# The up-projection of a feed-forward block as seven half-size products (Strassen's scheme), in three token blocks instead of two

## The chip, the cores and the metric

The kernel runs on one core of one Trainium2 chip. The metric is the device time in microseconds (us) of one execution; lower is better. The chip's engines run beside each other, each with its own queue in program order: TensorE (PE in the profile) multiplies matrices into PSUM, VectorE (DVE), ScalarE (ACT) and GpSimd (POOL) work elementwise, and transfers are queued by SyncE (SP) or POOL.

## What is computed

One layer of a hybrid decoder over 2048 prompt tokens and 8 x 8 sample tokens. Three mixers read one combined projection, their outputs are projected, added and layer-normed to x1; then comes a gated feed-forward block. The change is in that last block alone (and in how x1 is laid out for it):

```python
def conv_ffn(x, buf, w_up, conv_w, conv_b, w_down):
    up = x @ w_up                                   # 1024 -> 2 * 2816
    gate, val = jnp.split(up, [D_FF], axis=-1)
    gate, buf_new = causal_dwconv(gate, buf, conv_w)    # width 3, along the tokens
    h = jax.nn.gelu(gate + conv_b) * val
    return h @ w_down, buf_new                      # 2816 -> 1024
...
    f, fconv_new = conv_ffn(x, st_fconv, ffn_w_up, ffn_conv_w, ffn_conv_b, ffn_w_down)
    x = layer_norm(ALPHA * x + f, ln2_g, ln2_b)
```

All of it is float32. Every float32 product is made of three single passes (`mm3`): both operands are split into a rounded part (h, type fp32r) and the rest (l), and h\*h, l\*h and h\*l are added up in PSUM. To split is one ACT cast (h) and one subtraction on DVE or POOL (l = source - h).

## The kernel before

`program` (L1946) runs four stages: `phase1` (the combined projection), `window_a` (mixer A), `window_c` (mixer C beside the output projection, `Project`) and `phase3` (the feed-forward block). In `phase3` the program order is the order of the code (`manual_schedule`); each engine takes its instructions in that order.

**Tiles and loops.** The 2112 tokens are two blocks (`FB`): 1024 tokens, and 1024 + 64. The 2816 hidden columns are 22 tiles of 128 (`NH`). For each block and each hidden tile, `hidden` makes the gate rows and the value rows of the tile: a gate and a value product for each chunk of the block's tokens (512, 512 in the first block, 384, 384, 320 in the second), each product 8 steps of 128 in K by 3 passes, so 24 matmuls (`up`, PSUM tiles pug and puv, six banks in all). ACT copies the gate from PSUM to G (L1695), `conv` applies the three taps (one ACT activation L1713 and two DVE scalar_tensor_tensor L1715 to act) and the gelu (L1717), DVE multiplies with the value out of PSUM (L1748), ACT rounds to hh (L1749), DVE makes hl (L1757).

**Down-projection.** Hidden tiles are taken in pairs (`GRP` = 2). The products of a pair with `w_down` (`down`, PSUM tile pd, two banks) are queued behind the up-products of the tile that follows the pair: for each 128 tokens and each half of the 1024 columns, 2 x 3 matmuls, and one DVE add of the bank to Y (L1866 the first time, L1868 after). So the order on PE is: products of an even tile, down-products of the pair before it, products of the odd tile, products of the next even tile, and so on. I call the products of one tile P and one such run of down-products D. The tail of the even tile (the multiplication, hh, hl) is queued amid D's adds. A pair waits in hh and hl.

**Weights.** Weights are streamed for each block: `more` splits the next weight tile of 1024 columns (ACT cast L1605, POOL subtraction L1606 to wl_g, wl_v, wl_d) and queues the load of a later one on SP. The order `keys` is made ahead.

**Block change.** `load_x` (L1657 to L1659) loads and splits the tokens of a block in eight steps amid the down-products of the last pair of the block before. The second layer norm of a finished block (`stats`, `ln_scale`, `apply` L1779, `store`) is a list `todo`, from which `side` takes two or three entries at places in the next block's first tiles. `load_y` loads the x1 tile to which the down-products are added.

## Time and profile before

| | before |
|---|---|
| median of 3 runs | 3038.6 us (3037.53 to 3039.21) |
| profiled execution, its span | 3039.2 us |
| PE busy | 2895.7 us (95%), 17755 matmuls |
| DVE busy | 1597.9 us (53%) |
| ACT busy | 1231.6 us (41%) |
| POOL busy | 843.4 us (28%) |
| moved to and from memory | 80 GB/s over the span |

The profiled execution took as long as the runs (0.6 us over the median). PE, DVE and so on are engines, L1606 is a line of the kernel; a row names the line, the engine, the operation and the tiles as output<-inputs. In a timeline each row begins with the start and the duration in us, "x8" means eight instructions in a row merged, and a bracket holds the idle time before and what ended it. In the chain of waits, each row has the start, the time spent and the line. In a table of stages (windows) each engine has its busy time and, after x, its instructions; PEclk is the granted clock of TensorE, 1.00 at full speed. Matmuls are pipelined: their pace is read from the distance of two starts, not from one duration.

### The profile page before, as it was taken

What the parts mean: (1) busy time and instruction counts of PE and PEld (TensorE: products, weight loads), DVE (VectorE), ACT (ScalarE), POOL (GpSimd) and SP (SyncE); (2) the same over time, 40 slices, a digit from 0 to 9 for tenths busy, and PEclk for the clock granted to TensorE, in tenths of its full rate; (3) what the DMA queues carried; (4) which work ended last, traced back from release to release, by engine and by line L of the source; (5) the groups of instructions that cost most, each with busy time, mean ns of one, the idle gap of its engine ahead of it and who ended that gap; (6) DMA issues with size and microseconds to landing.
All of it is one profiled execution on the core that took longest, in us unless ns stands there. A gap on an engine that the chain in (4) does not pass through costs nothing.

```text
span 3039.2 us, 44833 instructions
## 1 busy us (share of the span) xinstructions
PE 2895.7 (95%) x17755; PEld 2496.9 (82%) x17755; DVE 1597.9 (53%) x2654; ACT 1231.6 (41%) x2591; POOL 843.4 (28%) x892
## 2 busy tenths in 40 slices
PE   8999999789889899998899999999999999999998
PEld 7888789678778677776678888888889999999997
DVE  4564442587665688978533333333366444334446
ACT  4474443446665567756332222222232222222223
POOL 0000001734523545434322222222232222222224
PEclk9999999689898679999999999999999999999999
DMA  6221112433433333322431111111124111111111
GB/s 197 83 74 70 56 61 100 137 106 107 123 99 91 81 120 109 111 82 87 160 123 50 49 42 63 42 56 42 49 104 152 42 47 51 49 42 42 48 43 62
DMA packets 182106, 247.20 MB, mean 81 GB/s; under 512 B 37986, under 2 KB 147640, under 8 KB 181832
## 3 DMA queue, kind: packets, MB, share of 16 engines
q1 hardware_dynamic: 179768, 237.02, 24.2%
q0 software_dynamic: 1984, 7.12, 0.6%
q8 instruction: 140, 2.29, 0.3%
q14 instruction: 70, 0.57, 0.1%
q10 hardware_dynamic: 144, 0.20, 0.0%
HBM read 183.94 MB, written 60.08 MB: 80 GB/s over the span
## 4 chain that ended last, share of the span: by engine, by line
PE 79%; DVE 10%; ACT 4%; issue 3%; DMA 2%; POOL 2%; SPq 0%; POOLq 0%; ACTq 0%; DVEq 0%
PE pm L320 20%; PE pd L320 15%; PE pug L320 15%; PE puv L320 15%; PE s L1364 2%; PE zp L1121 1%; DVE Tm L897 1%; DVE y L1779 1%; DVE tmp L895 1%; DVE K L1337 1%; PE zp L1122 1%; ACT WU L920 1%; PE zp L1123 1%; PE pd L1861 1%; DMA fxl<-s_x1T 1%
## 5 line engine op out<-in xcount | busy, mean ns | idle before, releaser
L1715 DVE SCALAR_TENSOR_TENSOR act<-G,cols,act 128x1024 f32<-128x1024 f32 (+1 forms) x132 | 123.6, 950 | 493.5 <-ACT act L1713 491.1
L1868 DVE TENSOR_TENSOR y<-y,pd 128x512 f32<-128x512 f32 x322 | 220.9, 687 | 203.3 <-PE pd L320 196.8
L1606 POOL TENSOR_TENSOR wl_d<-ws_d,wh_d 128x1024 fp32r<-128x1024 f32 x44 | 106.2, 2415 | 571.3 <-ACT wh_d L1605 547.3
L320 PE MATMUL pd<-wh_d,hh 128*128 128x512 f32 x704 | 215.8, 391 | 4.4 <-DVE y L1868 2.6
L320 PE MATMUL pd<-wh_d,hl 128*128 128x512 f32 x704 | 215.4, 391 | 0.0
L320 PE MATMUL pd<-wl_d,hh 128*128 128x512 f32 x704 | 214.9, 390 | 0.0
L1695 ACT COPY G<-pug 128x512 f32<-128x512 f32 (+2 forms) x110 | 55.2, 503 | 386.3 <-PE pug L320 386.3
L320 PE MATMUL pug<-fxh,wh_g 128*128 128x512 f32 (+2 forms) x880 | 197.0, 352 | 5.3 <-ACT fxh L1658 2.7
L320 PE MATMUL pug<-fxl,wh_g 128*128 128x512 f32 (+2 forms) x880 | 196.6, 352 | 2.5 <-POOL fxl L1659 1.5
L320 PE MATMUL puv<-fxh,wl_v 128*128 128x512 f32 (+2 forms) x880 | 197.1, 353 | 1.1 <-POOL wl_v L1606 1.1
L320 PE MATMUL puv<-fxh,wh_v 128*128 128x512 f32 (+2 forms) x880 | 197.1, 353 | 0.0
L320 PE MATMUL puv<-fxl,wh_v 128*128 128x512 f32 (+2 forms) x880 | 196.9, 352 | 0.0
L320 PE MATMUL pug<-fxh,wl_g 128*128 128x512 f32 (+2 forms) x880 | 196.2, 352 | 0.3 <-POOL wl_g L1606 0.3
L320 PE MATMUL pm<-xh,wh 128*128 128x448 f32 (+1 forms) x800 | 181.9, 360 | 8.3 <-ACT xh L370 6.7
L1605 ACT CAST wh_d<-ws_d 128x1024 fp32r<-128x1024 f32 x44 | 45.7, 1039 | 339.1 <-PE pd L1861 174.9
L320 PE MATMUL pm<-xh,wl 128*128 128x448 f32 (+1 forms) x800 | 181.7, 359 | 0.0
L320 PE MATMUL pm<-xl,wh 128*128 128x448 f32 (+1 forms) x800 | 180.0, 358 | 0.1
L1757 DVE TENSOR_TENSOR hl<-act,hh 128x512 fp32r<-128x512 f32 (+2 forms) x110 | 124.1, 1128 | 99.5 <-ACT hh L1749 99.5
L320 PEld LDWEIGHTS pug<-fxh,wh_g 128*128 128x128 f32 x880 | 156.2, 188 | 21.7 <-ACT fxh L1658 4.3
L320 PEld LDWEIGHTS pug<-fxl,wh_g 128*128 128x128 f32 x880 | 155.7, 188 | 16.9 <-POOL fxl L1659 2.0
L320 PEld LDWEIGHTS puv<-fxh,wl_v 128*128 128x128 f32 x880 | 156.1, 189 | 15.3 <-POOL wl_v L1606 1.3
L320 PEld LDWEIGHTS pm<-xh,wh 128*128 128x128 f32 x800 | 144.6, 188 | 28.9 <-issue 10.1
(731 smaller groups left out, 6371.0 us busy)
## 6 DMA issues: line engine op xcount, KB each, us to landing
ws_d<-in_w_dn SPq DMA_DIRECT2D x44, 512.0 KB
ws_g<-in_w_up SPq DMA_DIRECT2D x43, 512.0 KB
ws_v<-in_w_up SPq DMA_DIRECT2D x43, 512.0 KB
zx<-in_xT SPq DMA_DIRECT2D x56, 256.0 KB
ws<-in_w_in SPq DMA_DIRECT2D x19, 512.0 KB
x<-in_x SPq DMA_DIRECT2D x16, 512.0 KB
s_x<-x SPq DMA_DIRECT2D x16, 512.0 KB
s_x1T<-xt SPq DMA_DIRECT2D x16, 512.0 KB
```

Of the source, the lines that this page charges most:

```text
L320: nc.tensor.matmul(ps, w[k], x[k], start=first and i == 0, stop=last and i == 3 * n - 1)
L895: nc.vector.tensor_tensor(t, Y[:, j + 1:, j:j + 1].to_broadcast([128, k, j + 1]), Tm[:, j:j + 1, :j + 1].to_broadcast([128, k, j + 1]), op ...
L897: nc.vector.tensor_tensor(Tm[:, j + 1:, :j + 1], Tm[:, j + 1:, :j + 1], t, op=OP.subtract)
L920: nc.scalar.copy(o[:, h, :, :, jh * 32:(jh + 1) * 32], Ut[r, :, :3 * mt].rearrange("p i (a c) -> p a c i", a=3)[:, :, g.c0:g.c0 + m])
L1121: nc.tensor.matmul(ps, wh[:, k], xl, start=k == 0, stop=False)
L1364: nc.tensor.matmul(ps[64:, c], K[:, i], Q[:, i], start=True, stop=True)
L1605: nc.scalar.copy(h, t)
L1606: nc.gpsimd.tensor_tensor(lo, t, h.bitcast(F32), op=OP.subtract)
L1695: nc.scalar.copy(G[:, 2 + o:2 + o + m], p[:, :m])
L1715: nc.vector.scalar_tensor_tensor(dst(act), src(i), taps[i], dst(act), op0=OP.mult, op1=OP.add)
L1757: nc.vector.tensor_tensor(dst, act[:, c], hh[:, c].bitcast(F32), op=OP.subtract)
L1868: nc.vector.tensor_tensor(y, y, ps, op=OP.add)
```

## The change

Three things change in `phase3`, and the layout of x1 in memory with them.

**Seven products instead of eight halves.** For a hidden tile, the weights are seen as a 2 x 2 matrix of blocks A: gate and value tile (128 columns each) by the two halves of K (512 each). The tokens of a block are a 2 x 2 matrix B: the halves of K by the two halves of the block's tokens. Strassen's scheme in Winograd's form makes the four result blocks (gate and value, first and second half of the tokens) with seven products of half size in place of eight. A product is now 4 steps in K by 3 passes, 12 matmuls, over 384 tokens in the first two blocks and 288 in the third:

```python
PRODUCTS = [("A11", "B11"), ("S1", "T1"), ("S2", "T2"), ("S4", "B22"), ("S3", "T3"), ("A12", "B21"), ("A22", "T4")]
```

S1 to S4 are sums and differences of weight blocks, T1 to T4 of token blocks. The four weight sums (`wsum`) are made by DVE in place in the loaded weights (tiles r1 to r4, 128 x 512 each), and each of the seven weight operands is then split (`wsplit`: ACT cast; subtraction on DVE for S2 and S3, on POOL for the other five). All of it happens during the products of the tile before. The four token sums and seven splits are made once per block (`prepare_x`, 22 steps of 128 x 768 or 128 x 576, the subtractions on DVE and POOL). The seven results are combined out of PSUM: `hidden` copies products 0 and 1 by ACT (to G and p5) and adds the others by DVE to u and G, in the order of the products; one of the additions (p5 += u, both in SBUF) is on POOL. Gate rows end in G, value rows in u and p5, so the multiplication with the value (now L1831, L1833) reads SBUF.

**Three blocks instead of two.** `FB` is now 768, 768 and 512 + 64 tokens. Weights of the up- and the down-projection are therefore loaded and split three times. D is 12 steps of 6 matmuls in the first two blocks, and 8 of 6 and 2 of 4 in the third. Block changes are two.

**Down weights in halves.** `down_w` and `down_step` load and split w_down in pieces of 128 x 512 (ACT, POOL), two for each hidden tile, at places within `hidden`.

On DVE the rows between the adds of two D's show what a hidden tile now asks of it. Before, for the tile pair 15 and 16 of the second block (act, hl, hh tiles of hidden tile 15, y the sums, pd down-products):

```order
L1868 TENSOR_TENSOR y_8_20347<-y_8_20347,pd_12_81_23576 128x512
L1715 SCALAR_TENSOR_TENSOR act_15_23589<-G_15_23588,cols,act_15_23589 128x1024 x2
L1715 SCALAR_TENSOR_TENSOR act_15_23589<-G_15_23588,cols,act_15_23589 128x64 x2
L1748 TENSOR_TENSOR act_15_23589<-act_15_23589,puv_15_0_23688 128x384
L1757 TENSOR_TENSOR hl_15_23591<-act_15_23589,hh_15_23590 128x384
L1748 TENSOR_TENSOR act_15_23589<-act_15_23589,puv_15_1_23722 128x384
L1757 TENSOR_TENSOR hl_15_23591<-act_15_23589,hh_15_23590 128x384
```

And now, the even tile 18 of the third block (tile 62 of all), from the split of S2 to the first add of the D behind it (r1 to r4 raw weights of tile 63, wS2 and wS3 their split operands, pu4 to pu6 products in PSUM, u and G the running sums):

```order
L1629 TENSOR_TENSOR wS2_63l_28713<-r1_63_28584,wS2_63h_28712 128x512
L1635 TENSOR_TENSOR r2_63_28563<-r3_63_28590,r1_63_28584 128x512
L1781 TENSOR_TENSOR u62_28636<-u62_28636,pu4_62_28717 128x288
L1635 TENSOR_TENSOR r1_63_28584<-r4_63_28614,r1_63_28584 128x512
L1781 TENSOR_TENSOR G2_18_28631<-G2_18_28631,pu5_62_28739 128x288
L1629 TENSOR_TENSOR wS3_63l_28754<-r1_63_28584,wS3_63h_28753 128x512
L1781 TENSOR_TENSOR u62_28636<-u62_28636,pu6_62_28767 128x288
L1747 SCALAR_TENSOR_TENSOR act2_18_28632<-G2_18_28631,cols_76,act2_18_28632 128x512 x2
L1747 SCALAR_TENSOR_TENSOR act2_18_28632<-G2_18_28631,cols_76,act2_18_28632 128x64 x2
L1949 TENSOR_TENSOR y2_0_25377<-y2_0_25377,pd2_16_00_28796 128x512
```

The weight sums and two of the weight splits of the next tile now stand on DVE between the additions of the products, and the taps of the even tile still stand ahead of the first add of D. Ahead of these rows stand the sums S1 and S2 and the earlier additions to u and G.

On POOL, the splits of a tile before (wl_g, wl_v and wl_d of 1024 columns, fc the carried columns of the convolution):

```order
L1606 TENSOR_TENSOR wl_d_15_23683<-ws_d_15_23380,wh_d_15_23682 128x1024
L1606 TENSOR_TENSOR wl_g_16_23714<-ws_g_16_23586,wh_g_16_23713 128x1024
L1606 TENSOR_TENSOR wl_v_16_23780<-ws_v_16_23686,wh_v_16_23779 128x1024
L1710 COPY fc<-G_16_23785 128x16
L1711 COPY fc<-G_16_23785 128x2
```

And now (wA and wS weight operands of tile 64, wdl the down weights, p the sum p5):

```order
L1629 TENSOR_TENSOR wA_64l<-r_64_28757,wA_64h 128x512
L1629 TENSOR_TENSOR wS_64l<-r_64_28736,wS_64h 128x512
L1666 TENSOR_TENSOR wdl_28879<-r_18_0_28882,wdh_28878 128x512
L1781 TENSOR_TENSOR p_28888<-u_28889,p_28888 128x288
L1629 TENSOR_TENSOR wS_64l<-r_64_28736,wS_64h 128x512
L1629 TENSOR_TENSOR wA_64l<-r_64_28763,wA_64h 128x512
L1666 TENSOR_TENSOR wdl_28881<-r_19_0_28948,wdh_28880 128x512
L1629 TENSOR_TENSOR wA_64l<-r_64_28785,wA_64h 128x512
L1742 COPY fc<-G_19_28884 128x16
```

Three instructions of 1024 columns for a tile of 1024 or 1088 tokens have become seven of 512 and one of 288 (384) for a tile of 576 (768) tokens.

The core of the diff:

```diff
-FB = [(0, 1024, 0, (512, 512)), (1024, 1024, 64, (384, 384, 320))]
+FB = [(0, 768, 0), (768, 768, 0), (1536, 512, 64)]
...
+        SUMS = {"S1": ("r2", "r4", OP.add), "S2": ("r2", "r1", OP.subtract), "S4": ("r3", "r1", OP.subtract),
+                "S3": ("r4", "r1", OP.subtract)}
...
+        def parts(src, e, name):
+            h, lo = (wp.tile([128, 512], F32R, tag=f"u{x}", bufs=NSLOT, name=name + x) for x in "hl")
+            nc.scalar.copy(h, src)
+            e.tensor_tensor(lo, src, raw(h), op=OP.subtract)
+            return h, lo
+
+        def wsum(i, nm):
+            if i < len(hs):
+                a, b, op = SUMS[nm]
+                nc.vector.tensor_tensor(R[i, OPS[nm]], R[i, a], R[i, b], op=op)
+
+        def wsplit(i, nm):
+            if i < len(hs):
+                W[i, nm] = parts(R[i, OPS[nm]], nc.vector if nm in ("S2", "S3") else nc.gpsimd, f"w{nm}_{i}")
...
+        def down_step():
+            if halves:
+                ht, j, t = halves.pop(0)
+                h, lo = D[ht][j]
+                nc.scalar.copy(h, t)
+                nc.gpsimd.tensor_tensor(lo, t, raw(h), op=OP.subtract)
+                down_load(0)
...
+            for f, nm, i, e in ((xsum, "T1", 0, v), (xsum, "T1", 1, v), (xsplit, "B11", 0, v), (xsplit, "B11", 1, v),
+                                (xsum, "T3", 0, g), (xsum, "T2", 0, v), (xsplit, "T1", 0, v), (xsum, "T3", 1, g),
+                                (xsum, "T2", 1, v), (xsplit, "T1", 1, v), (xsplit, "T2", 0, v), (xsplit, "T2", 1, v),
+                                (xsplit, "B22", 0, g), (xsplit, "B22", 1, g), (xsplit, "T3", 0, v), (xsum, "T4", 0, v),
+                                (xsum, "T4", 1, v), (xsplit, "T3", 1, v), (xsplit, "B21", 0, g), (xsplit, "B21", 1, g),
+                                (xsplit, "T4", 0, g), (xsplit, "T4", 1, g)):
+                yield
+                f(nm, i, e)
...
+            v, g = nc.vector, nc.gpsimd
+            wsplit(i + 1, "A11")
+            nc.scalar.copy(g1, product(0))
+            side(3)
+            nc.scalar.copy(p5, product(1))
+            wsum(i + 1, "S1")
+            add(v, u, g1, product(2))
+            wsum(i + 1, "S2")
+            wsplit(i + 1, "S1")
+            for o, f in g2:
+                add(v, o, f(u), f(p5))
+            down_step()
+            side(2)
+            p = product(3)
+            for o, f in g2:
+                add(v, o, o, f(p))
+            wsplit(i + 1, "S2")
+            wsum(i + 1, "S4")
...
+            add(v, u, u, product(4))
+            add(g, p5, u, p5)
+            wsplit(i + 1, "S4")
+            load_raw(i + 2, "r2")
+            wsum(i + 1, "S3")
...
+            add(v, g1, g1, product(5))
+            wsplit(i + 1, "S3")
+            load_raw(i + 2, "r1")
+            wsplit(i + 1, "A12")
+            load_raw(i + 2, "r3")
+            down_step()
+            add(v, u, u, product(6))
+            wsplit(i + 1, "A22")
+            load_raw(i + 2, "r4")
+            conv(bi, ht, G, act)
...
+            yield hh, hl
+            nc.vector.tensor_tensor(act[:, :w], act[:, :w], u, op=OP.mult)
+            nc.scalar.copy(hh[:, :w], act[:, :w])
+            nc.vector.tensor_tensor(act[:, w:n], act[:, w:n], p5, op=OP.mult)
+            nc.scalar.copy(hh[:, w:n], act[:, w:n])
+            yield
+            nc.vector.tensor_tensor(hl[:, :np_], act[:, :np_], raw(hh[:, :np_]), op=OP.subtract)
...
-                Y[tt] = tr.tile([128, DM], F32, tag="y", bufs=9, name=f"y{bi}_{tt}")
+                Y[tt] = tr.tile([128, DM], F32, tag="y", bufs=6, name=f"y{bi}_{tt}")
...
                 if pend is not None:
+                    if pend[0] == 0:
+                        side(len(todo))
+                        load_y(bi, 0, Y)
                     for _ in down(bi, pend, H, Y, pend[0] == 0, tail):
                         pass
...
+                px = prepare_x(bi + 1)
+                for _ in range(5):
+                    next(px)
+                for _ in down(bi, pend, H, Y):
+                    next(px, None), next(px, None)
```

Y has six buffers now, so the layer norm of a finished block has to be stored before the next block's first D begins: what is left of `todo` is queued there.

More of the change, by code (lines that the diff above doesn't have):

```diff
@@ L1759, in phase3 @@
-        mv = pool.tile([128, 9, 2], F32, name="l2mv")
+            w = n // 2
+            end = i == len(hs) - 1
+            change = ht == NH - 1 and not end
+            G = tr.tile([128, 776], F32R, tag="G", name=f"G{bi}_{ht}").bitcast(F32)
+            act = tr.tile([128, 768], F32, tag="act", bufs=1, name=f"act{bi}_{ht}")
+            if not end:
+                hh = tr.tile([128, 768], F32R, tag="hh", bufs=GRP + 1, name=f"hh{bi}_{ht}")
+                hl = tr.tile([128, 768], F32R, tag="hl", bufs=GRP + 1, name=f"hl{bi}_{ht}")
@@ new lines, in hidden, with product @@
+            p5 = tr.tile([128, HW], F32, tag="p5", bufs=1, name=f"p5{i}")[:, :w]
+            u = tr.tile([128, HW], F32, tag="u", bufs=1, name=f"u{i}")[:, :w]
+            def product(j):
+                a, b = PRODUCTS[j]
+                ps = pu.tile([128, 512], F32, tag="pu", name=f"pu{j}_{i}")[:, :w]
+                wh, wl = W.pop((i, a))
+                xh, xl = X[bi, b]
+                mm3(nc, ps, [wh[:, q * 128:(q + 1) * 128] for q in range(4)],
+                    [wl[:, q * 128:(q + 1) * 128] for q in range(4)],
+                    [xh[:, q] for q in range(4)], [xl[:, q] for q in range(4)],
+                    by_k=ht == 0)
+                if change:
+                    load_x(bi + 1, b)
+                return ps
@@ L1855, in down @@
                         ps = pd.tile([128, 512], F32, tag="pd", name=nm)
-                    ws = [[W[f"d{bi}_{ht}"][a][:, js] for ht in hts] for a in range(2)]
+                    ws = [[D[ht][j][a] for ht in hts] for a in range(2)]
                     if m < 128:
@@ L1876, in fold @@
             if m < 128:
-                t = tr.tile([128, 1088], F32, tag="act", bufs=1, name=f"fold{bi}")
-                nc.scalar.copy(t[:m, :DM], Y[tt][m:])
-                nc.gpsimd.tensor_tensor(Y[tt][:m], Y[tt][:m], t[:m, :DM], op=OP.add)
-        more()
-        for X in load_x(0):
+                t = tr.tile([128, DM], F32, tag="y", bufs=6, name=f"fold{bi}")
+                nc.scalar.copy(t[:m], Y[tt][m:])
+                nc.gpsimd.tensor_tensor(Y[tt][:m], Y[tt][:m], t[:m], op=OP.add)
+        for _, b in PRODUCTS:
+            load_x(0, b)
+        for r in ("r1", "r2", "r4", "r3"):
+            load_raw(0, r)
+        nc.vector.memset(carry, 0.0)
+        wsplit(0, "A11")
+        wsum(0, "S1")
+        wsum(0, "S2")
+        wsplit(0, "S1")
+        wsplit(0, "S2")
+        px = prepare_x(0)
+        for _ in range(13):
+            next(px)
+        wsum(0, "S4")
+        wsplit(0, "S4")
+        load_raw(1, "r2")
+        wsum(0, "S3")
+        wsplit(0, "S3")
+        load_raw(1, "r1")
+        wsplit(0, "A12")
+        load_raw(1, "r3")
+        wsplit(0, "A22")
+        load_raw(1, "r4")
+        for _ in px:
             pass
-        more()
+        down_w(range(GRP))
         nc.sync.dma_start(sfc, E.d["s_fconv"])
@@ L1891, in phase3 @@
             for ht in range(NH):
-                tail = hidden(bi, ht, X)
+                tail = hidden(bi, ht)
                 H[ht] = next(tail)
```

245 lines of the change are left out of this document (105 added, 140 removed).

## The prediction

> **What bounds the kernel now.** I read the page first, then the table of stages, then the chain of waits. The page:
>
> ```profile
> span 3039.2 us, 44833 instructions
> PE 2895.7 (95%) x17755; PEld 2496.9 (82%) x17755; DVE 1597.9 (53%) x2654; ACT 1231.6 (41%) x2591; POOL 843.4 (28%) x892
> ```
>
> The table of stages, for the two long stretches of the feed-forward block (PE, PEld, DVE, ACT, POOL busy, granted clock, DMA):
>
> ```profile
> 1600.00:2200.00 600.00, 600.00 (x2647) 496.53 (x2646) 212.87 (x259) 137.93 (x182) 142.91 (x73) 1.00 0.14 48
> 2300.00:2970.00 670.00, 668.14 (x3686) 628.27 (x3685) 274.11 (x381) 162.04 (x287) 152.20 (x97) 1.00 0.15 53
> ```
>
> PE is busy all the time at full clock, DVE for 35 to 41%, POOL for 24%: here fewer matmuls are less time as long as the others keep up. The chain of waits through the stage, with the block change in its middle and the end:
>
> ```profile
> 1585.97 21.80 PE pd L320 x96
> ...
> 2206.67 10.88 PE puv L320 x48
> ...
> 2341.52 11.84 PE pug L320 x72
> ...
> 2388.94 21.80 PE pd L320 x96
> 2412.72 11.84 PE pug L320 x72
> ...
> 2970.41 11.86 PE puv L320 x72
> 2982.27 11.05 PE pd L320 x48
> ```
>
> PE passes from P to D without a break (2970.41 + 11.86 = 2982.27). Two P's of the second block take 2388.94 - 2341.52 = 47.4, a D of it 23.8. From 2217.55 to 2341.52 lie a D (21.8), three P's (71.1) and a D (23.8): 116.7 of 124.0, so the block change costs 7.3. The first D begins at 1585.97 behind three P's of 21.76 (below): the stage runs as if from 1520.7 without a break.
>
> **Products.** The pace of matmuls of 512, 384 and 320 columns, from starts eight apart:
>
> ```profile
> 1629.38 1.98 PE L320 MATMUL pug<-fxh,wh_g 128*128 128x512 f32 x8
> 1631.20 1.98 PE L320 MATMUL pug<-fxh,wl_g 128*128 128x512 f32 x8
> 2342.76 1.55 PE L320 MATMUL pug<-fxh,wl_g 128*128 128x384 f32 x8
> 2344.14 1.55 PE L320 MATMUL pug<-fxl,wh_g 128*128 128x384 f32 x8
> 2350.85 1.34 PE L320 MATMUL pug<-fxh,wl_g 128*128 128x320 f32 x8
> 2352.03 1.33 PE L320 MATMUL pug<-fxl,wh_g 128*128 128x320 f32 x8
> ```
>
> That is 0.227, 0.173 and 0.147 us each; the step of 0.053 over 128 columns puts 288 columns at 0.133 (estimate; its upper bound, no gain below 320, would cost 22 x 84 x 0.014 = 25). Before, a hidden tile costs 96 x 0.2267 + 96 x 0.1733 + 48 x 0.1465 = 45.4, now 84 x (0.1733 x 2 + 0.1332) = 40.3; by 22 tiles **-112**. P is 14.56 in the first two blocks and 11.2 in the third, a product 2.08 and 1.6. The down-products are the same 2112 + 88 matmuls; D is now 72 x 0.227 = 16.3.
>
> **What DVE and POOL now do in that shorter time.** Durations (the groups by form, then single rows of the timeline):
>
> ```profile
> L1715 DVE SCALAR_TENSOR_TENSOR act<-G,cols,act 128x1024 f32<-128x1024 f32 x88 | 113.0, 1284 | 492.7 <-ACT act L1713 491.1
> L1715 DVE SCALAR_TENSOR_TENSOR act<-G,cols,act 128x64 f32<-128x64 f32 x44 | 12.4, 282 | 0.8
> L1748 DVE TENSOR_TENSOR act<-act,puv 128x384 f32<-128x384 f32 x44 | 24.0, 546 | 22.4 <-ACT act L1717 22.4
> L1868 DVE TENSOR_TENSOR y<-y,pd 128x512 f32<-128x512 f32 x322 | 220.9, 687 | 203.3 <-PE pd L320 196.8 <-PE pd L1861 5.1
> L1171 DVE BATCH_NORM_STATS2 l2st<-y 128x6 f32<-128x512 f32 x16 | 10.0, 664 | 0.0
> L1089 POOL TENSOR_TENSOR xl<-zx,xh 128x512 fp32r<-128x512 f32 x56 | 74.0, 1335 | 114.8 <-ACT xh L1088 95.6 <-issue 14.8 <-DMA kv<-s_v 1.7
> L1802 POOL TENSOR_TENSOR y<-y,l2g 128x704 f32<-128x704 f32 x7 | 12.0, 1715 | 20.7 <-ACT y L1799 20.7
> 2114.76 0.69 DVE L1757 TENSOR_TENSOR hl<-act,hh 128x512 fp32r<-128x512 f32 x1
> 2292.46 0.75 DVE L1779 SCALAR_TENSOR_TENSOR y<-y,l2mv,l2g 128x512 f32<-128x512 f32 x1
> ```
>
> By these, in between by proportion: a DVE tensor_tensor of 512, 384, 288 columns 0.69, 0.55, 0.44; the taps 1.02 (768) or 0.75 + 0.28 (512 + 64) each; a POOL subtraction of 512 columns 1.34, of 384 and 288 1.08 and 0.89, of 768 1.84. What they do to each other shows at the second block's first D, in the timeline of DVE, POOL and PE and the stage's clock:
>
> ```profile
> 2313.79 1.51 DVE L1757 TENSOR_TENSOR hl<-act,hh 128x384 fp32r<-128x384 f32 x1 [1.57 <-ACT hh L1749]
> 2316.35 1.61 DVE L1757 TENSOR_TENSOR hl<-act,hh 128x384 fp32r<-128x384 f32 x1 [0.58 <-ACT hh L1749]
> 2317.89 1.27 DVE L1866 SCALAR_TENSOR_TENSOR y<-y,pd 128x512 f32<-128x512 f32 x2
> 2312.48 2.42 POOL L1606 TENSOR_TENSOR wl_g<-ws_g,wh_g 128x1024 fp32r<-128x1024 f32 x1 [8.84 <-ACT wh_g L1605]
> 2314.84 2.70 POOL L1606 TENSOR_TENSOR wl_v<-ws_v,wh_v 128x1024 fp32r<-128x1024 f32 x1
> 2234.38 0.73 PE L320 MATMUL pd<-wh_d,hh 128*128 128x512 f32 x2 [2.15 <-DVE y L1868]
> 2318.61 0.98 PE L320 MATMUL pd<-wh_d,hh 128*128 128x512 f32 x2 [1.85 <-DVE y L1866]
> 2318.90:2322.30 3.40, 3.40 (x9) 2.66 (x9) 1.34 (x3) 0.46 (x1) 0.00 (x0) 0.50 1.04 418
> ```
>
> This is the change's stall in small. A subtraction of 384 columns from SBUF, 0.55 by itself, takes 1.51 and 1.61: each ends 0.4 behind the end of the POOL instruction it met (2314.90, 2317.54). So a DVE instruction with both inputs in SBUF and a POOL instruction exclude each other; one that reads PSUM does not care (L1748 has its 0.55 throughout). DVE comes 2 us late to the adds of D, both pd banks are full, PE waits 1.85 before the third step, and then runs at half clock for 3.4, which costs another 1.7.
>
> [...]
>
> *First and second block.* From the start of the P of an odd tile DVE has: a wait for product 2 (6.24), then five adds from PSUM (2.75), five weight instructions (3.45), G (0.55), taps (2.04), two multiplications (1.10), hl (0.96): 10.85; then the even tile's S1 and the same up to its taps, 9.48; the first add of D, 0.69. Sum 27.3. POOL has meanwhile 12 splits of 512 and 2 sums: 18.2, of which at most 5.5 lie beside the PSUM adds: +12.7. Back: 0.15 for each of 14 meetings (2.1), and 0.09 for each of 33 instructions, since successive ones overlap (two adds of 0.69 take 1.27), 3.0. The add ends at 34.9. PE needs it at 2 P + 2 steps of D = 31.8. PE stalls 3.1 (bounds: 0.6, when DVE only follows product 6 with its add, the taps and the first add of D, ending at 32.4; 8.2, without what I took back). Half clock after it: the pause at 2318 brought it, that of 2.15 at 2234 did not, so half of 1.7, 0.85. There are 10 such D's in the first block and 9 in the second, 19 x 3.95 = **+75**.
>
> *Third block.* Wait 4.8; 10.46 and 9.34 in the same way (the samples' rows add two instructions to G, two to the taps, one to hl); add 0.69: 25.3. POOL 18.6, less 4.9 beside, +13.7; back 5.8. The add ends at 33.2, needed at 22.4 + 2.7 = 25.1: stall 8.1 (bounds 0.5, 13.9), half clock 1.7; 8 D's, **+78**.
>
> *Layer norm of the block before.* It must be done before the first D of a block, within three P's: six tiles, each with two statistics of 0.66 and four scalings of 0.75, 26, with small ones 27.2, all in DVE's queue, and Y is loaded again behind it (a load such as this took 6.8 at most, I take 4):
>
> ```profile
> 1489.02 6.81 DMA fxl<-s_x1T
> ```
>
> Second block: 6.24 + 31.9 for three tiles + 27.2 + 4 + 0.69 = 70, POOL 30 less 8 beside, back 11: 80.7 against 43.7 + 2.7: 34. Third: 4.8 + 31.0 + 27.2 + 4 + 0.69, POOL 31 less 7.4, back 11.5: 79.7 against 36.3: 43. With half clock **+81** (bounds 39 without POOL's share, 100).
>
> *Block changes.* D of the last pair stands right behind its odd tile, so PE waits for taps, gelu, hh and hl: 6.24 + 10.85, POOL's 9.1 less 2.75, back 2.5, gelu and hh 1.3: hl is there at 22.3 of 14.56, 7.5 late (the gelu lies between). In D, DVE has 14 token steps of 0.96 besides 12 adds: 3.84 before the first, 14.4 up to the eighth, then PE's pace 6.8, and POOL's 8 steps add 6: 14 late. The third block's steps are 576 wide: 8 late. With half clock 2 x 1.7, together **+40** (20 to 50); the 7.3 of before go, **-7**.
>
> *End.* Three P's stand without a D before the last one: DVE has 4.8 + 10.5 + 11.1 + 7.0, POOL adds some 10, gelu and hh 1.3: 45 of 33.6; with half clock **+13** (6 to 16). *Start.* PE's first product now stands behind the transposes of the last tile of x1, and POOL has 8 token steps and 4 splits (20) and DVE 17.6, mostly excluding each other. The last group of the output projection ends at 1500.3,
>
> ```profile
> 1498.34 1.98 PE L320 MATMUL pm<-wol,mh 128*128 128x512 f32 x8
> ```
>
> its layer norm takes some 5, the token steps 20 to 33: product 6 runs at 1525 to 1538, as if from 1513 to 1525, against 1520.7: **+3** (-8 to +10). Loads are 1.5 MB for a tile of 17.5 to 22.7, under 90 GB/s where the block change already moves 418; I cost them at nothing, ACT (10 us of a P of 14.6) too.
>
> Sum: -112 + 75 + 78 + 81 + 40 - 7 + 13 + 3 = +171, on the profiled 3039.2 **3210 us**. The median of the runs is 0.6 lower; a measurement tells about 0.2%, 6 us.
>
> **Rivals.** *The waits between DVE and POOL are absorbed* (POOL's splits fall where DVE waits for PE). For it: POOL waits for ACT's casts, and DVE idles 6.2 at each odd tile. Against: every meeting in the rows costs. Then each term stands at its lower bound: 19 x 0.6 + 8 x 0.5 = 15, layer norm 39, changes 20 - 7, end 6, start 2: -112 + 75 = -37, **3002**. It decides where the sum of the stalls passes 112. *Half of the waits are absorbed*: in the first two blocks the add then comes at 29.6 of 32.4 and the stall is 0.6 (11 in all); in the third 2.3 + 1.7 (32); layer norm 58, changes 30 - 7, end 9, start 3: +24, **3063**. *Idle TensorE loses its clock less often than taken.* The row shows it lost behind a pause of 1.85; then 19 x 0.85 + 11 x 1.7 = 35 too much, 3175. [...]
>
> **How the numbers follow.** The exclusion is seen at every meeting and the queues are fixed, so the forecast has 0.52, the clock kept oftener 0.10, half absorbed 0.18, absorbed 0.20. The first case's own range is 3110 to 3310 (bounds of the steady stalls and the layer norm). Over all I take 2995 to 3310, which leaves out about half of the absorbed case and the worst of the first. Faster 0.23, from the absorbed case and the lower edge of the half one; same 0.04; slower 0.73.
>
> **What would show it.** Right: the pace of P's matmuls 0.173 and 0.133; single subtractions on DVE at 1.2 to 1.7 instead of 0.69; PE idle before the third step of nearly every D, waiting for DVE's add, 3 us in the first two blocks and 8 in the third; two long gaps of 30 to 40 at the first D of a block; mean PE clock below 0.95 in the stage. Wrong: DVE's subtractions near 0.7 beside a busy POOL, PE over 97% busy from 1540 on, or PE waiting for weights within P rather than at D, which my sums do not hold.

## The result, and the profile after

The changed kernel takes 3353.3 us (median of 4 runs, 3352.1 to 3353.9), the kernel before 3038.1 beside it: ratio 1.1042, 95% interval 1.1027 to 1.1058. The direction was forecast, the size was not: 3210 was the forecast and 3310 the upper end of the range. The profiled execution has a span of 3351.1, 311.9 more than the one of before.

The head of the page, and then the stage in four stretches (PE, PEld, which is the loading of weights into TensorE, DVE, ACT, POOL busy, granted clock, DMA share and GB/s). The first goes from the first to the ninth steady D of the first block (steady: neither the first nor the last D of a block), the last from the first to the eighth of the third:

```profile
span 3351.1 us, 49037 instructions
PE 2900.2 (87%) x18019; PEld 2519.1 (75%) x18019; DVE 2252.3 (67%) x3556; ACT 1454.5 (43%) x3151; POOL 1335.4 (40%) x1317
```

```profile
1644.64:2068.38 423.74, 389.02 (x1921) 352.08 (x1921) 284.31 (x369) 139.43 (x257) 202.22 (x144) 0.95 0.18 60
2106.21:2276.40 170.19, 116.92 (x566) 104.13 (x565) 128.97 (x163) 56.60 (x97) 76.49 (x51) 0.85 0.25 87
2739.93:2894.52 154.59, 97.40 (x549) 86.58 (x549) 121.22 (x175) 51.20 (x103) 67.28 (x54) 0.82 0.27 89
2894.52:3236.57 342.05, 275.63 (x1571) 241.64 (x1569) 252.92 (x380) 119.45 (x254) 170.54 (x141) 0.87 0.20 65
```

Each stretch begins and ends with the start of a D. The first holds eight pairs of 52.97 us (a D and the two P's behind it), where 45.4 is the time without a wait (2 x 14.56 + 16.3); the last holds seven of 48.86, where it is 35.1 (2 x 11.2, and 56 matmuls at 0.227). The two in the middle are the block changes, from the last D of a block to the first steady one of the next. PE's clock was 1.00 in the same stage before.

What PE waits for, from the table of waits (total in us, how often, the longest), and the start of one D in the first block, in PE's timeline, with the start of the odd tile's P behind it:

```profile
PE pd L320 <- DVE y L1947: 64.3, 3, 26.2
PE pd L320 <- ACT wdh L1665: 62.3, 26, 6.1
PE pd L320 <- POOL wdl L1666: 61.6, 26, 2.8
PE pd L320 <- DVE y L1949: 36.8, 32, 1.9
```

```profile
1859.37 0.50 PE L320 MATMUL pd<-wdh,hh 128*128 128x512 f32 x1 [0.79 <-ACT wdh L1665]
1863.37 0.50 PE L320 MATMUL pd<-wdl,hh 128*128 128x512 f32 x1 [2.81 <-POOL wdl L1666]
1864.78 1.22 PE L320 MATMUL pd<-wdh,hh 128*128 128x512 f32 x2 [0.91 <-DVE y L1949]
1865.80 1.05 PE L320 MATMUL pd<-wdh,hl 128*128 128x512 f32 x2
...
1880.04 0.86 PE L320 MATMUL pu<-xB11h,wA_13h 128*128 128x384 f32 x4
```

The second step of D waits for the second half of the down weights, the third for DVE's add, and the two matmuls behind that take 1.02 (1864.78 to 1865.80) where 0.46 is full clock. A reader of the table alone would say that the down weights are the cause, 124 us against 37 for DVE. In the third block the same three waits come to 9.2 us in place of 4.5, though the second of them is shorter:

```profile
2950.99 0.80 PE L320 MATMUL pd<-wdh,hh 128*128 128x512 f32 x1 [5.88 <-ACT wdh L1665]
...
2954.46 0.80 PE L320 MATMUL pd<-wdl,hh 128*128 128x512 f32 x1 [1.40 <-POOL wdl L1666]
2957.13 1.22 PE L320 MATMUL pd<-wdh,hh 128*128 128x512 f32 x2 [1.87 <-DVE y L1949]
```

DVE's groups in the eight pairs of the first block (count, then busy time and mean ns of one):

```profile
L1635 DVE TENSOR_TENSOR r<-r,r 128x512 f32<-128x512 f32 x64 | 54.8, 855 | 4.3 <-DMA r<-in_w_up 4.3
L1747 DVE SCALAR_TENSOR_TENSOR act<-G,cols,act 128x768 f32<-128x768 f32 x32 | 52.3, 1635 | 11.3 <-ACT act L1745 10.7
L1781 DVE TENSOR_TENSOR G<-G,pu 128x384 f32<-128x384 f32 x32 | 17.7, 552 | 7.3 <-PE pu L320 5.6
L1781 DVE TENSOR_TENSOR G<-u,p 128x384 f32<-128x384 f32 x16 | 17.5, 1097 | 0.0
```

The last two rows are the same addition of 384 columns. With one input in PSUM it takes 0.55, with both in SBUF 1.10 in the mean.

### The profile page after: what moved, and what is told of

It reads as the page before. It is cut to its first block, busy times and chain, and to the rows that moved or that the text cites. A ratio compares the mean times of both kernels' runs of the same rounds, so it can differ in the third digit from the quotient of the medians.

```text
span 3351.1 us, 49037 instructions
## 1 busy us (share of the span) xinstructions
PE 2900.2 (87%) x18019; PEld 2519.1 (75%) x18019; DVE 2252.3 (67%) x3556; ACT 1454.5 (43%) x3151; POOL 1335.4 (40%) x1317
## 5 line engine op out<-in xcount | busy, mean ns | idle before, releaser
L320 PE MATMUL pd<-wdh,hh 128*128 128x512 f32 x688 | 257.7, 453 | 192.0 <-DVE y L1947 64.3
L320 PEld LDWEIGHTS pd<-wdh,hh 128*128 128x128 f32 x688 | 145.6, 219 | 247.3 <-ACT wdh L1665 73.5
L320 PE MATMUL pd<-wdl,hh 128*128 128x512 f32 x688 | 248.8, 439 | 61.6 <-POOL wdl L1666 61.6
L1747 DVE SCALAR_TENSOR_TENSOR act<-G,cols,act 128x768 f32<-128x768 f32 (+2 forms) x176 | 240.5, 1376 | 46.7 <-ACT act L1745 43.6
L320 PE MATMUL pd<-wdh,hl 128*128 128x512 f32 x688 | 240.6, 434 | 0.5 <-DVE hl L1836 0.5
L1635 DVE TENSOR_TENSOR r<-r,r 128x512 f32<-128x512 f32 x264 | 223.9, 848 | 21.5 <-DMA r<-in_w_up 10.4
L320 PEld LDWEIGHTS pd<-wdl,hh 128*128 128x128 f32 x688 | 146.2, 213 | 108.9 <-POOL wdl L1666 75.2
L1666 POOL TENSOR_TENSOR wdl<-r,wdh 128x512 fp32r<-128x512 f32 x128 | 217.3, 1697 | 14.0 <-ACT wdh L1665 14.0
L320 PEld LDWEIGHTS pd<-wdh,hl 128*128 128x128 f32 x688 | 147.8, 215 | 36.3 <-DVE hl L1836 1.9
L320 PEld LDWEIGHTS pm<-xh,wl 128*128 128x128 f32 x800 | 144.5, 188 | 20.4 <-issue 9.9
```

What stands on the lines that cost most here:

```text
L320: nc.tensor.matmul(ps, w[k], x[k], start=first and i == 0, stop=last and i == 3 * n - 1)
L1635: nc.vector.tensor_tensor(R[i, OPS[nm]], R[i, a], R[i, b], op=op)
L1666: nc.gpsimd.tensor_tensor(lo, t, raw(h), op=OP.subtract)
L1747: nc.vector.scalar_tensor_tensor(dst(act), src(i), taps[i], dst(act), op0=OP.mult, op1=OP.add)
```

## The experiments

Every run is compared with the kernel before on the same chip. Three runs leave a part of the computation out, to measure its cost: no_pool and pool_copy the low parts that POOL makes, no_ln the layer norm of two blocks. A pair is the distance from the start of one D to that of the next in PE's timeline, the mean of eight in the first block and of seven in the third. The row without a wait holds for seven products; plain3 has longer P's, and without a wait its pairs would take 49.6 (192 x 0.1733 + 16.3) and 38.3 (192 x 0.1332 + 12.7).

| run | median us | ratio to before (95%) | pair, first block | pair, third block |
|---|---|---|---|---|
| no wait at all | | | 45.4 | 35.1 |
| changed kernel | 3353.3 | 1.104 (1.103 to 1.106) | 53.0 | 48.9 |
| down_early | 3397.1 | 1.119 (1.117 to 1.122) | 55.1 | 50.3 |
| no_pool | 3089.5 | 1.018 (1.016 to 1.020) | 46.4 | 39.0 |
| all_dve | 3338.9 | 1.100 (1.098 to 1.102) | 53.8 | 47.0 |
| plain3 | 3146.4 | 1.037 (1.035 to 1.038) | 50.9 | 42.5 |
| taps_late | 3287.7 | 1.083 (1.081 to 1.084) | 50.2 | 46.9 |
| no_ln | 3301.1 | 1.087 (1.086 to 1.089) | 53.2 | 48.8 |
| pool_copy | 3119.4 | 1.027 (1.025 to 1.029) | 46.7 | 40.5 |
| warm | 3318.9 | 1.094 (1.092 to 1.095) | 51.1 | 48.9 |
| order2 | 3273.7 | 1.078 (1.077 to 1.080) | 50.5 | 46.7 |
| stored | 3193.6 | 1.051 (1.049 to 1.053) | 56.6 | 39.7 |
| stored2 | 3139.3 | 1.035 (1.032 to 1.037) | 55.3 | 36.0 |
| stored3 | 3108.4 | 1.023 (1.022 to 1.025) | 52.5 | 36.2 |

My theory was that DVE comes late to D because its subtractions and POOL's exclude each other. The rivals: the down weights are late (the table of waits); DVE's own queue is too long, whatever POOL does; three blocks as such cost the time.

**Down weights earlier** (down_early).

```diff
             nc.scalar.copy(p5, product(1))
+            if ht % 2 and not change:
+                down_step()
...
-            down_step()
+            if ht % 2 or change:
+                down_step()
             add(v, u, u, product(6))
```

> The four half tiles of the down weights of a pair are split one, two and three places earlier (three in the odd tile, one in the even). Theory (DVE comes late to the first add of D; the weights are only late beside it): in the first two blocks the third step of D then starts when DVE has made its add, 0.9 us or less before where it starts now, in the third 1.9 at most: 19 x 0.9 + 8 x 1.9 = 32 at the very most, and POOL's earlier work pushes DVE back, so 3320 to 3360 us, with the idle time of PE now put down to DVE y. Rival (the rows of waits, 62 us for ACT wdh and 62 for POOL wdl, are what bounds D): 124 less, 3230.

```profile
PE pd L320 <- DVE y L1952: 203.1, 32, 9.4
PE pd L320 <- DVE y L1950: 66.1, 3, 26.8
```

The 124 us for the down weights are gone from the table, and 203 for DVE's add stand in their place (37 before). So the rival is refuted. The time rose by 44, more than I allowed. In the pair from 1949.10 on the first add begins 38.3 behind the start of the odd tile, where it was 36.4 in the changed kernel; 1.1 of that are longer waits of DVE, the rest longer instructions. The longest new wait comes from ACT's queue:

```profile
1958.62 0.62 ACT L1665 CAST wdh<-r 128x512 fp32r<-128x512 f32 x1 [3.58 <-DMA r<-in_w_dn]
1959.80 1.42 DVE L1629 TENSOR_TENSOR wS_16l<-r,wS_16h 128x512 fp32r<-128x512 f32 x1 [0.99 <-ACT wS_16h L1628]
```

ACT's cast of the down weights, moved ahead, waits for their load, and the cast of wS_16h that DVE needs stands behind it. That POOL's earlier work pushes DVE back, as I had expected, can be at most the other 0.8. Down weights and add had come late together, and the table puts a wait down to whichever is needed first.

**POOL's weight subtractions left out** (no_pool).

```diff
         def parts(src, e, name):
+            if e is nc.gpsimd:
+                h = wp.tile([128, 512], F32R, tag="uh", bufs=NSLOT, name=name + "h")
+                nc.scalar.copy(h, src)
+                return h, h
...
-                nc.gpsimd.tensor_tensor(lo, t, raw(h), op=OP.subtract)
```

> POOL's subtractions for weights are left out (the rounded part stands in for the rest in the matmuls, so the low parts of five up operands and of w_down are missing from the products); the same matmuls, ACT casts and DVE instructions. Theory (POOL's subtractions and DVE's with two SBUF inputs exclude each other): DVE's subtractions take 0.69 again, the first add of D ends 27 us behind the start of the odd tile where PE needs it at 31.9, and the steady stalls (7.4 each in the first two blocks, 13.3 in the third, 239 in all) fall to 0 to 1 in the first two and 1 to 4 in the third; with 20 to 40 less at the layer norm: 3090 to 3150. Rival 1 (DVE's own queue is too long, POOL doesn't matter): within 40 of 3353. Rival 2 (ACT's casts come late): the same, with PE waiting for ACT.

```profile
1630.12:2001.71 371.59, 367.27 (x1921) 340.63 (x1921) 234.35 (x368) 139.36 (x257) 23.04 (x32) 1.00 0.21 69
```

```profile
L1639 DVE TENSOR_TENSOR r<-r,r 128x512 f32<-128x512 f32 x64 | 43.9, 685 | 0.0
L1750 DVE SCALAR_TENSOR_TENSOR act<-G,cols,act 128x768 f32<-128x768 f32 x32 | 32.5, 1016 | 0.6
```

264 us less, and the same eight pairs at full clock. DVE's instructions are as many as before (x368 and x369), but DVE is busy for 234.35 and not 284.31: 6.2 us of a pair were DVE instructions made longer by POOL's. A tap takes 1.02, not 1.64. That an instruction itself gets longer no wait for data explains. DVE's in-place sums could also have to wait until POOL has read; in the changed kernel's table of DVE's waits for the eight pairs no wait for POOL stands.

**All weight subtractions on DVE** (all_dve).

```diff
-                W[i, nm] = parts(R[i, OPS[nm]], nc.vector if nm in ("S2", "S3") else nc.gpsimd, f"w{nm}_{i}")
+                W[i, nm] = parts(R[i, OPS[nm]], nc.vector, f"w{nm}_{i}")
...
-                nc.gpsimd.tensor_tensor(lo, t, raw(h), op=OP.subtract)
+                nc.vector.tensor_tensor(lo, t, raw(h), op=OP.subtract)
```

> All weight subtractions on DVE, none on POOL (p5 + u stays on POOL). Theory (exclusion): each of the 12 of a pair then takes DVE 0.60 where POOL's kept DVE's work out for 1.3 to 1.7; 7.2 for some 10 to 12, so the add comes 1 to 4 earlier at each D: 3250 to 3330. Rival (DVE's length of work alone counts, POOL works beside it for nothing): 7.2 later at each of 27 D's and in the stretches of the layer norm: 3540 or more.

14 less (interval of the ratio below the changed kernel's), just outside what I expected (3330), and 200 away from the rival. To give DVE fourteen subtractions for each pair of tiles more costs no more than to have POOL make them: POOL's help was worth nothing. In the first block a pair is 0.8 longer, in the third 1.8 shorter.

**POOL copies in place of subtractions** (pool_copy).

```diff
-            e.tensor_tensor(lo, src, raw(h), op=OP.subtract)
+            if e is nc.gpsimd:
+                e.tensor_copy(lo, raw(h))
+            else:
+                e.tensor_tensor(lo, src, raw(h), op=OP.subtract)
...
-                nc.gpsimd.tensor_tensor(lo, t, raw(h), op=OP.subtract)
+                nc.gpsimd.tensor_copy(lo, raw(h))
```

> POOL's subtractions for weights become copies of the same size, one input from SBUF instead of two (the low parts are then not the differences). If only POOL instructions with two inputs keep DVE's out: as with the subtractions left out, 3090 to 3130. If any POOL instruction does: as long as the copy takes as long as the subtraction, 3353, and in proportion below it (half as long: 3200 to 3240).

POOL's copy and a DVE subtraction, alone and meeting each other:

```profile
1889.89 0.68 DVE L1632 TENSOR_TENSOR wS_16l<-r,wS_16h 128x512 fp32r<-128x512 f32 x1
...
1894.05 1.13 DVE L1632 TENSOR_TENSOR wS_16l<-r,wS_16h 128x512 fp32r<-128x512 f32 x1
```

```profile
1894.02 0.61 POOL L1630 CAST wA_16l<-wA_16h 128x512 fp32r<-128x512 f32 x1
1894.58 1.07 POOL L1669 CAST wdl<-wdh 128x512 fp32r<-128x512 f32 x1
```

By its time this run would say that copies don't exclude (3119, in the first of my ranges). The rows show the same as with subtractions: where they meet, DVE's takes 1.13 for 0.68, and a copy of POOL 1.07 for 0.61. But a copy takes 0.61 where a subtraction takes 1.3 to 2.0. Of one pair, DVE's share up to the first add, here and with the subtractions left out (no_pool):

```profile
1880.89:1912.99 32.10, 32.04 (x181) 31.19 (x179) 21.80 (x32) 14.99 (x27) 12.56 (x17) 1.00 0.27 87
1879.69:1911.54 31.85, 31.85 (x181) 31.19 (x179) 20.11 (x33) 14.98 (x27) 2.92 (x4) 1.00 0.28 89
```

The copies make DVE's instructions 1.7 longer (21.80 - 20.11), but DVE's waits get 1.4 shorter (11.7 to 10.3), so the add comes only 0.25 later. The time isn't in proportion to POOL's, as I had put it.

**Taps behind the first adds** (taps_late: with the early down weights).

```diff
                 nc.scalar.activation(dst(act), src(0), AF.Identity, scale=taps[0], bias=col("fcb", ht))
+            yield
+            for src, dst in parts:
                 for i in (1, 2):
...
             yield hh, hl
+            next(cv, None)
+            yield
```

> The early down weights of the run before, and in addition the two DVE taps of a tile that a D follows stand behind the first two adds of that D instead of ahead of them; the same instructions. Theory (what PE waits for is the place of the first add in DVE's queue): the add comes by the taps' 3.3 us earlier (4.3 in the third block), so D's go from 25.6 to about 22 in the first two blocks and from 24.5 to about 20 in the third; that is 2 less than in the changed kernel 19 times and 6 less 8 times: about 3265 us (3230 to 3300). Rival (DVE and POOL together have more work in a pair than the pair's time, so order is worth nothing and the wait moves elsewhere): 3380 or more, as with the early down weights alone.

3288: in the range, and 109 below the run with the early weights alone. The steady D's of the first block take 21.1 (22 expected). The pair of the third block is 2 shorter than in the changed kernel where I expected 6: its D's take 21, but its two P's 25.7 in the mean, 3.0 more than before. Order counts: there is room for the taps in D, and the two moves together gain where the one alone lost.

**TensorE kept busy in the pause** (warm).

```diff
+        def warm(n, a, b):
+            ps = pu.tile([128, 512], F32, tag="pu", name="warm")
+            for i in range(n):
+                nc.tensor.matmul(ps, a, b, start=True, stop=True)
...
+                    if tail is not None and not first and tt == 0 and j == 1:
+                        warm(36 if ns else 18, H[hts[0]][0][:, ts], D[hts[0]][0][0])
```

> The changed kernel with TensorE kept busy while it waits: ahead of the second step of each steady D stand 18 matmuls (36 in the third block) on operands that are ready, into a PSUM tile that nobody reads. DVE, ACT and POOL have the same work. Theory (a D loses its pause and then 3 us in the first two blocks, 4 in the third, to TensorE at half clock behind the pause): the pauses are filled, the half clock goes with them, 18 x 3 + 8 x 4 = 86 less at best, and the extra matmuls overshoot the pause by up to 0.5: 3267 to 3300, with the granted clock at 1.00 in the steady D's. Rival (the lower clock is not due to the pause, or D is bound by DVE's adds all the way so that PE's pace is not what counts): within 10 of 3353, or above it.

```profile
1851.99 4.28 PE L1925 MATMUL warm<-wdh,hh 128*128 128x512 f32 x18
...
1858.66 0.72 PE L320 MATMUL pd<-wdh,hh 128*128 128x512 f32 x2 [0.91 <-DVE y L1956]
```

```profile
1646.14:2055.09 408.95, 401.67 (x2065) 367.09 (x2065) 289.16 (x369) 139.51 (x257) 202.84 (x144) 1.00 0.19 62
2864.24:3206.27 342.03, 322.51 (x1823) 284.76 (x1822) 253.76 (x379) 118.54 (x252) 171.21 (x141) 0.96 0.20 65
```

34 less by work that nobody reads. In the first block the clock is 1.00 and a pair 1.85 shorter (52.97 - 51.12), and 18 x 1.85 is the gain: that is the half clock by itself, in the steady D's of the first two blocks. The 3 us that I expected were too many. In the third block the clock is 0.96, waits for DVE's add of up to 2.3 stayed in the run, and the pair is as long as before: there the split between wait and clock stays open.

**Layer norm left out, and spread** (no_ln, order2). The first stores the sums of two blocks as they are; the second is taps_late with each tile's store and the next load taken tile by tile:

```diff
-                    if pend[0] == 0:
-                        side(len(todo))
-                        load_y(bi, 0, Y)
+                        need_y(bi, 0, Y)
...
+        def need_y(bi, tt, Y):
+            while tt not in Y and todo:
+                side(1)
```

> The layer norm of the first two blocks is left out (their sums are stored as they are); all else as in the changed kernel. Theory (the long wait at the first D of the second and third block, 26 us each, is for the layer norm's 27 us on DVE that stand ahead of it): both waits go but for that of a steady D, and the P's ahead lose their waits of 10 and 18 in part: 60 to 85 less, 3268 to 3293. Rival (the wait is for the sums of tokens left over from the block change, or for loading the rows): above 3320.

> The run with late taps and early down weights, and in addition the layer norm of the block before is taken tile by tile: each finished tile is stored and the next block's sums loaded behind it, and the steps that are left are queued amid the first D and not all ahead of it. Theory (what PE waits for at the first D of a block is that all of it stands ahead of the first add): 15 to 40 of the 52 that leaving it out gave: 3248 to 3273. Rival (DVE has no room for it in D either, the wait moves into the D): 3280 or more.

No layer norm: 52 less, short of 60 to 85. At the second block's first D PE still waits:

```profile
2205.83 1.22 PE L320 MATMUL pd<-wdh,hh 128*128 128x512 f32 x2 [11.93 <-DVE y L1947]
```

```profile
2205.09 1.28 DVE L1947 SCALAR_TENSOR_TENSOR y<-y,pd 128x512 f32<-128x512 f32 x2 [3.89 <-DMA y<-s_x]
```

DVE is late there as at any D, and then waits 3.9 for the load of the rows. Spread: 14 less than taps_late, at the edge of what I expected.

**Three blocks without Strassen** (plain3): the kernel before with other numbers in `FB`.

```diff
-FB = [(0, 1024, 0, (512, 512)), (1024, 1024, 64, (384, 384, 320))]
+FB = [(0, 768, 0, (384, 384)), (768, 768, 0, (384, 384)), (1536, 512, 64, (288, 288))]
```

> The kernel before in three blocks of 768, 768 and 512 + 64 tokens, with its eight halves as before and no Strassen. Theory (the loss lies in the work on DVE and POOL that the seven products ask for): matmuls of 384 and 288 columns cost 22 x 0.7 = 15, a block change more 7 to 15: 3058 to 3075, PE above 97% busy in the stage. Rival (three blocks as such, by weights streamed a third time and layer norms that must be done within three tiles, cost the larger part of the 312): 3150 or more.

```profile
PE pug L320 <- POOL wl_g L1607: 49.2, 34, 2.7
```

```profile
1654.17 1.67 PE L320 MATMUL pug<-fxh,wl_g 128*128 128x384 f32 x8 [0.97 <-POOL wl_g L1607]
...
2736.09 1.32 PE L320 MATMUL pug<-fxh,wl_g 128*128 128x288 f32 x8 [2.71 <-POOL wl_g L1607]
```

My expectation fell: 3146, near the rival's 3150. Three blocks cost 110 us without Strassen (3036.4 beside it), 15 of them for shorter matmuls (by the paces of the prediction, a tile in all three blocks takes 192 x 0.1733 + 96 x 0.1332 = 46.07, before 45.4). In shorter P's POOL's split of the gate weights comes late, 1 us in each pair of the first two blocks and 2.7 in the third. Against this kernel Strassen in the same three blocks saves 127 us of matmuls (22 x (46.07 - 40.3)) and costs 207 net.

**Weight work once** (stored, stored2, stored3). The first block stores its split operands, the others load them:

```diff
+            if i < NH:
+                t, *W[i, nm] = parts(R[i, OPS[nm]], nc.vector if nm in ("S2", "S3") else nc.gpsimd, f"w{nm}_{i}")
+                keep(lambda: nc.sync.dma_start(wst[i][NAMES.index(nm)], raw(t)))
+            elif i < len(hs):
+                keep()
+                t = slot(f"w{nm}_{i}")
+                nc.sync.dma_start(raw(t), wst[hs[i][1]][NAMES.index(nm)])
```

stored2 adds the order of order2, stores queued later and down weights loaded at once; stored3 queues the stores on ACT (`nc.scalar.dma_start`).

> Only the first block sums and splits weights; it also stores the split operands (3.7 MB for a hidden tile, 1 MB of down weights) to memory, and the second and third block load them, without weight work on DVE, POOL and ACT. Theory (that work, done three times, is the loss): steady D's fall from 24 to 17.5 or less in the second block and from 26 to 13.5 in the third, 62 + 101 less; the changes of blocks and the end 20 to 60 less: 3120 to 3170. Rival (4.7 MB for each tile of 17 to 23 us, 210 to 270 GB/s, can't be brought in time): PE waits for operands within P, 3250 or more.

> The run with stored operands, with four edits of order: taps behind the first adds of D and early down weights in the first block, stores queued three operands behind their making, the stored down weights loaded all at once behind D, and the layer norm's last steps and the loads of the next sums taken tile by tile amid the first D. Theory (in the run before, stores that wait on SP's queue for a subtraction held back the raw weights behind them, so the first block's D's rose from 24 to 27.5; in the third block D waited for down weights loaded too late): first block's D's 21 to 22 (9 x 6 less), third block's 13.5 to 14.5 (8 x 3.5 less), layer norm 20 to 45 less: 3065 to 3100. Rival (the memory traffic itself holds the first block back): its D's stay at 25 or more and the time above 3130.

> The run before of the stored operands, with the first block's stores queued by ACT and not by SP, nothing else changed. Theory (in that run a store on SP's queue waits for POOL's subtraction, up to 17 us, and the raw weights queued behind it come 5 us late to DVE's first sum of each pair): the first block's D's fall from 26 to 21 or 22, 10 x 4.5 = 45 less: 3085 to 3105, still above the kernel before. Rival (the memory traffic of the stores slows the loads, whichever queue): D's at 25 or more, 3130 or above.

stored2, the steady pairs of the second and third block, and DVE's waits in its first block:

```profile
2280.56:2652.70 372.14, 367.22 (x1921) 340.57 (x1921) 178.82 (x272) 61.01 (x112) 18.40 (x32) 1.00 0.58 204
2794.69:3046.54 251.85, 247.69 (x1571) 227.36 (x1569) 134.32 (x294) 49.49 (x127) 14.91 (x42) 1.00 0.69 263
```

```profile
DVE u L1814 <- PE pu L320: 40.3, 8, 5.0
DVE r L1649 <- DMA r<-in_w_up: 37.3, 8, 5.4
```

SP's queue in stored2 (start and time of each issue), and DVE's waits for raw weights and for ACT's part of the taps in stored3:

```profile
1869.64 0.98 SPq L1654 DMA_DIRECT2D wst<-wS  x2
1870.72 0.99 SPq L1629 DMA_DIRECT2D r<-in_w_up  x1
```

```profile
DVE r L1649 <- DMA r<-in_w_up: 4.9, 5, 1.5
DVE act L1780 <- ACT act L1776: 32.7, 16, 3.5
```

Without weight work a pair takes 46.5 and 36.0, 1 us over no wait, at full clock, and 263 GB/s are moved beside it. What stored and stored2 missed of their expectation (3194 for 3120 to 3170, 3139 for 3065 to 3100) lies in the first block, whose pairs rose to 57 and 55, and in stored also in the third (39.7), where PE waits for stored down weights. DVE waits 5 us in each pair for raw weights, whose loads stand on SP's queue among eleven stores for a tile, of which those shown take 0.5 each to issue. With the stores on ACT's queue that wait is 0.6 and the first block's pair takes 52.5; its D's take 23.4 (52.5 less the 29.1 of the P's), not the 21 to 22 expected, and 3108 is 3 over the range. What I had said of the stores, that they wait up to 17 us for POOL, is not in the rows: SP's longest waits for POOL in the first block, 15.2 in stored2 and 16.0 in taps_late, stand at the load of down weights, and the longest of a store is 3.9 in stored2. So the queue is shown to matter, not how. Part of the wait has moved with the stores: DVE now waits 32.7 us in the eight pairs for ACT's part of the taps, 10.7 in stored2. That is 2.75 more in a pair, on the queue that now issues the stores. This is the best version found with seven products, 2.3% slower than the kernel before.

## Why the prediction was wrong

It came out 141 us short (3351.1 against 3210). Step by step:

- *Products, -112: right.* Two P's that wait for nothing take 29.13 (168 x 0.1733); in stored2 22.1 in the third block (0.1317 for 288 columns, estimated 0.133).
- *Steady D's of the first two blocks, +75: the step that failed.* Measured: 52.97 - 45.4 = 7.6 for each of 18, and 16 for the very first: 153. Two things failed in it. "Sum 27.3 ... The add ends at 34.9": I laid POOL's delays upon the sum of DVE's work. But DVE takes the products as PE makes them and can't end the add before 32.4 (my lower bound). The 5.1 us between 27.3 and 32.4 are spent waiting for product after product, and few of them take up a delay; in the pair shown POOL meets DVE's two taps, the last work ahead of the add, and makes them 3.33 us in place of 2.04. The add began 36.4 behind the start of the odd tile (forecast 34.2). The row of that add, and the stretch from the start of the odd tile to it:

```profile
1916.42 1.27 DVE L1949 TENSOR_TENSOR y<-y,pd 128x512 f32<-128x512 f32 x2
1880.04:1916.42 36.38, 32.80 (x181) 31.22 (x179) 26.18 (x33) 14.98 (x27) 22.64 (x16) 0.99 0.22 72
```

  DVE works for 26.18 of it, 6.1 more than in no_pool (20.11, above): that is the delay, for which 12.7 - 2.1 - 3.0 = 7.6 was forecast, so it was somewhat too large. Its 2.1 of 0.15 for each meeting comes from the two rows of before, which leave 0.15 and 0.13 (1.11 to the end of POOL's row and 0.55 are 1.66 for 1.51, 1.19 and 0.55 are 1.74 for 1.61); in the changed kernel the DVE rows at 1887.03 (1.59) and 1904.90 (1.65) leave 0.14 and 0.13 in the same way, and for each of 14 meetings no run shows it. DVE waits for 10.2, where my sum had 6.24; of the 11.7 that it waits in no_pool only 1.5 took up a delay. And "half of 1.7, 0.85" for the clock: 1.85 by the run that filled the pause. So 3.95 should have been 5.7 + 1.85.
- *Third block, +78:* 13.8 for each of 8, 110. The same step (forecast 8.1 + 1.7): from the start of the odd tile at 2920.61 to the add at 2956.39 DVE waits 7.2, my sum had 4.8. Here the delay was too small as well: DVE works for 28.61 there, and in the mean of the seven pairs for 36.13 (252.92 / 7) and in no_pool for 26.19 (183.33 / 7), 9.9 more where 13.7 - 5.8 = 7.9 was forecast.
- *Layer norm and block changes, 81 + 40:* from the last D of a block to the first steady one there are 105.4 and 85.1 of matmuls in 170.19 and 154.59, so 134. Of it 47 lie in the last D's (42.4 and 37.7 long, 16.3 without a wait) and 87 in the three P's and the first D behind them, so both terms were nearly right. But what is called layer norm in the 81 is only in part the layer norm: leaving it out gives 52, and without it the first D's of the second and third block are still 14.8 and 14.2 longer than without a wait.
- *Start, +3:* 19. The first D starts at 1583.15 behind three P's of 43.7, as if from 1539.5, against 1520.7. DVE and POOL make the sums and splits of tokens there at the same time, and the DVE split shown takes 2.60 beside a POOL split from 1535.23 to 1537.79; it is worse than my bound of +10. The start of that D, and one of DVE's token splits, for which 0.96 was my term:

```profile
1583.15 1.05 PE L320 MATMUL pd<-wdh,hh 128*128 128x512 f32 x2
```

```profile
1536.01 2.60 DVE L1719 TENSOR_TENSOR xT3l<-tT,xT3h 128x768 fp32r<-128x768 f32 x1
```

- *End, +13:* 15, as what is left of 311.9; not measured by itself.

The rivals: "absorbed" and "half absorbed" are refuted, a quarter of the delay is absorbed in the first block (1.5 of 6.1). "Loses its clock less often than taken" went the other way, 1.85 for each D and not 0.85. The upper end of the range, 3310, was said to stand at the bounds of the steady stalls and the layer norm, but it doesn't: by the prediction's own bounds these are 19 x 5.1 + 8 x 5.8 + 19 = 162 above 3210, so 3372, and the measured 3351 lies below that. None of the named signs of being wrong was met; PE waits for weights, but at D and not within P, and the early down weights showed that this wait covered DVE's. Of the signs of being right one was off: the gaps at the first D of the second and third block are 26 us long, not 30 to 40; the P's ahead of them are already 9.6 and 18.6 late.

The cause of the loss is thus shown in its main part: leaving POOL's subtractions out takes 264 of the 315 us away, loading stored operands shows pairs within 1 us of the matmuls. Not all of it belongs to the seven products: three blocks as such, for which the prediction had no rival, cost the kernel of before 110. Not shown is how much of the third block's 13.8 is clock (9.2 are waits in the D shown, the rest slower matmuls and waits within P), and how much the stores on ACT's queue add to the first block's D's, 23.4 in the last run.

## What to carry to other kernels

When fewer matmuls are bought with elementwise work on weights, count that work on DVE and POOL as one queue wherever both read SBUF (here 3338.9 with all weight subtractions on DVE, 3353.3 with most of them on POOL), and against PE's pace in the shorter stage; work whose result is used again belongs in memory, not in every block (3193.6 stored, 3353.3 made in every block). A delay is to be laid upon the time at which an engine's inputs let it finish, not upon the sum of its work. A row of waits names what the waiting engine needs first; move that and look who stands behind it.
